# Eight small products of the mLSTM samples: one accumulation in one column tile, against four column tiles at once with the sum on VectorE

## The chip, the cores and the metric

The kernel runs on one core of a Trainium2 chip. The metric is the device time of one execution in microseconds (us), as the median of several timed runs. One execution was also recorded by the hardware profiler; everything said about where the time goes comes from that one trace. The engines carry the names PE (TensorE's matmuls), PEld (TensorE's weight loads), DVE (VectorE), ACT (ScalarE), POOL (GpSimd) and SP (the queue that issues most loads).

## What is computed

The program is one inference step of a two-layer decoder, for a prompt of 512 tokens and for eight separate samples of one token each. Layer 1 has an mLSTM mixer with four heads. For a sample, a head keeps a state C0 of 128 x 256. The part of the reference that the change touches, with t = 1 for the samples and b = 8, is:

```python
def mlstm_chunk(q, k, v, ig, logf, C0, n0, m0):
    ...
    s = jnp.einsum('bhtd,bhsd->bhts', q, k) * w
    num = g[..., None] * jnp.einsum('bhtd,bhde->bhte', q, C0) + jnp.einsum('bhts,bhse->bhte', s, v)
    den = g * jnp.einsum('bhtd,bhd->bht', q, n0) + jnp.sum(s, axis=-1)
    h = num / jnp.maximum(jnp.abs(den), jnp.exp(-m))[..., None]
    ...
    C = g_last[..., None, None] * C0 + jnp.einsum('bhs,bhsd,bhse->bhde', w_last, k, v)
```

Each sample has its own query and its own state, so the product of query and state is eight products of a 1 x 128 row with a 128 x 256 matrix, per head. After the mixer come an output projection, a layer norm, a mixture of 16 experts, a second layer norm and a gate, all on prompt and samples together.

## The kernel before

The mixer of layer 1 is the method `odd`. Its input projection runs as a stream of products `ws_steps`: the weights come in blocks of 128 output columns, ScalarE makes a rounded copy of each block (L137) and VectorE the remainder (L138), and TensorE runs 48 matmuls of 128 x 256 or 128 x 264 on them (L234). Everything else of the mixer is written as Python generators that are advanced once per block (`later`, `advance`), so that their instructions lie between the matmuls of the stream. The tile framework then orders the instructions of each engine by its own plan of when operands come free. Each engine takes its instructions strictly in that order.

`slots` sets which generator is put in when: for each head h it issues the two blocks of v, then `scores(h + 1)` and `sample_head(h, cin)`, and the blocks of o in between. `head(h)` is the prompt's part: for four chunks it computes hs (L1804, L1808, L1809) and updates the prompt's state C (L1811, L1813, and L1815 for the first chunk), and `norm_h` normalizes it (L1837 to L1848; POOL takes a power at L1845). `ocons` applies the gate (L1857, L1858).

`sample_head(h, cin)` is the samples' part, and the place of the change. `cin` holds the eight states of one head, 128 partitions (d) by eight samples by 256. `qm` (L1929) holds for each sample b a 128 x 8 matrix with the query of sample b in column b and zeros elsewhere. Line 1937 multiplies the eight of them with the eight states and lets them accumulate in one PSUM tile of 8 x 256, so that row b of the result is sample b. Lines 1939 and 1941 scale the result, add the term of the new value, and store `num`, a slice of `nums`. Then line 1949 makes the outer products of key and value and line 1950 updates `cin`, in pairs that share a PSUM tile. PSUM tiles named tps come from a pool of four (`tp`); a tile is given out again when its last reader is done.

`sample_out` follows when all four heads are done: `norm_h` on `nums`, eight transposes of it (L266), the gate (L1967). `mix_all` is the output projection, whose first matmuls L142, L143 and L144 need the split result yh and yl of VectorE's and ScalarE's last products, and split weights (L138).

Of the kernel before, what the change touches and what calls it, by code (L numbers as in the profile page):

```python
# [14 lines left out]
OP = mybir.AluOpType  # L15
# [6 lines left out]
NS = 8  # L22
# [98 lines left out]
class K:  # L121
# [1524 lines left out]
    def odd(self):  # L1646
        tc, nc, A, O = self.tc, self.nc, self.A, self.O
        V, S, G, TE = self.V, self.S, self.G, self.T
# [3 lines left out]
        with tc.tile_pool(name="mz", bufs=1) as mz, tc.tile_pool(name="mx", bufs=1) as mx, tc.tile_pool(name="mx2", bufs=2) as mx2:  # L1652
# [6 lines left out]
            ps = self.acc()  # L1659
            for k in range(8):  # L1660
                for z, (a, b) in enumerate(((self.wgh, self.xh), (self.wgh, self.xl), (self.wgl, self.xh))):
                    for q, (t0, t1) in ((ps[:8, 0, 256:512], HALF[0]), (ps[:8, 1, 0:T - 256], HALF[1])):
                        TE.matmul(q, a[:, k, :], b[:, k, t0:t1],
                                  start=(k == 0 and z == 0), stop=(k == 7 and z == 2))
# [4 lines left out]
            ps = self.tp()  # L1669
# [6 lines left out]
            ig, z = ga[:, :, 0:4], ga[:, :, 4:8]  # L1676
# [187 lines left out]
            inter, mm, ws_, gs, ems = (sm[:, z, :] for z in range(1, 6))  # L1864
# [60 lines left out]
            def sample_head(h, cin):  # L1925
                while h not in vdone or len(sdone) < h:
                    yield
                qm = p2.tile([128, 8, 8], F32, name="qm")
                V.tensor_tensor(qm, qT[:, h, None, TP:T].to_broadcast([128, 8, 8]),  # L1929
                                self.c("mask8").rearrange("p (a b) -> p a b", a=8), op=OP.mult)  # L1930

                kk = p2.tile([72, 8, 128], F32R, name="kk", bufs=1)
                V.tensor_tensor(kk, kst[:, None, chunk(h)].to_broadcast([72, 8, 128]).bitcast(F32),
                                self.c("bm")[:72, :, None].to_broadcast([72, 8, 128]), op=OP.mult)
                ps = self.tp()
                for b in range(NS):
                    TE.matmul(ps[:NS, :256], qm[:, b, :], cin[:, b, :], start=(b == 0), stop=(b == 7))
                num = nums[:, h, 0:256]
                V.tensor_scalar(num, ps[:NS, 0:256], gs[:, h:h + 1], None, op0=OP.mult)
                for r in (slice(0, NS), slice(32, 40)):  # L1940
                    V.scalar_tensor_tensor(num, vst[r, h, :].bitcast(F32), sm[:, 6, h:h + 1], num, op0=OP.mult, op1=OP.add)
                for b2 in range(4):
                    if h < 2 or b2 == 0:
                        yield
                    ps = self.tp()
                    for b in range(2):
                        bb = 2 * b2 + b
                        pb = ps[:, b * 256:(b + 1) * 256]
                        TE.matmul(pb, kk[:, bb, :], vst[:, h, :], start=True, stop=True)
                        V.scalar_tensor_tensor(cin[:, bb, :], cin[:, bb, :], gB[:, bb, h:h + 1], pb, op0=OP.mult, op1=OP.add)  # L1950
                G.dma_start(O["C_sample"][0, :, h].rearrange("b p v -> p b v"), cin)
                sdone.add(h)
# [19 lines left out]
            def slots():  # L1972
                self.later(maxima())
                self.later(sample_gates())
                yield from product(4, kcons, 4)
                yield from product(0, qcons, 4)
                self.later(sample_keys())
                self.later(scores(0))
                cins = [sample_load(h) for h in range(2)]
                for n, h in HORD:  # L1980
                    if n == "v":
                        yield from product(8 + 2 * h, vcons)
                        if h < 3:
                            self.later(scores(h + 1))
                        self.later(sample_head(h, cins[h]))
                        if 0 < h < 3:
                            cins.append(sample_load(h + 1))
                    else:
                        yield from product(16 + 2 * h, ocons)
# [57 lines left out]
```

## Time and profile before

| what | value |
|---|---|
| timed runs, median of 3 | 1394.33 us (1392.32 to 1396.9) |
| profiled execution, its own time | 1390.96 us |
| span from first to last instruction in it | 1389.1 us |
| TensorE matmul busy | 1267.9 us (91% of the span) |
| VectorE busy | 858.5 us (62%) |
| ScalarE busy | 627.9 us (45%) |
| GpSimd busy | 254.0 us (18%) |

The profiled execution took 1.9 us more than its span, and 3.4 us less than the median of the timed runs. The busy shares are averages over stages with different limits. The mixer of layer 1 lies between about 740 and 920 us of the span, its output projection begins at 920, and the experts of layer 1 run from about 1005 to 1305.

### The profile page before, as it was taken

How to read it: one execution, taken by the hardware profiler on the slowest of the kernel's cores; microseconds unless marked ns; L12 is line 12 of the kernel's file. 1: busy time of each engine (PE TensorE's matmuls, PEld its weight loads, DVE VectorE, ACT ScalarE, POOL GpSimd, SP SyncE). 2: the span in 40 equal slices, each digit the busy share in tenths (PEclk: the TensorE clock that was granted, in tenths of full speed). 3: DMA queues.
4: the chain of work that ended last, by engine and by line, in shares of the span. 5: the costliest groups of instructions: out<-in, count | busy, mean ns of one | idle time of the engine just before them, and what ended most of it. 6: DMA issues, size and time to landing. Idle time of an engine off the chain costs nothing. (4 is left out here: it accounts for less than half of the span.)

```text
span 1389.1 us, 20899 instructions
## 1 busy us (share of the span) xinstructions
PE 1267.9 (91%) x7884; PEld 967.1 (70%) x7884; DVE 858.5 (62%) x1503; ACT 627.9 (45%) x1053; POOL 254.0 (18%) x242
## 2 busy tenths in 40 slices
PE   8989988995899999888989999999589999999897
PEld 7988876563766655447979988878467565555686
DVE  4699976448976554437554465765788555444572
ACT  3224563224665444337553333233357555444562
POOL 1023312313111211001220000101311112110113
PEclk9999999997999999999999999999889999999999
DMA  8568636864999989997423313483389999999911
GB/s 282 157 221 303 220 137 245 304 240 164 350 359 368 350 301 368 365 363 215 128 86 93 92 46 114 164 324 127 130 304 327 371 361 315 344 371 339 307 56 40
DMA packets 157449, 338.73 MB, mean 244 GB/s; under 512 B 16095, under 2 KB 54459, under 8 KB 153246
## 3 DMA queue, kind: packets, MB, share of 16 engines
q1 hardware_dynamic: 138974, 271.28, 54.9%
q0 software_dynamic: 18224, 65.98, 15.3%
q8 instruction: 64, 1.05, 0.3%
q14 instruction: 43, 0.35, 0.1%
q10 hardware_dynamic: 144, 0.07, 0.0%
HBM read 313.66 MB, written 32.81 MB: 249 GB/s over the span
## 5 line engine op out<-in xcount | busy, mean ns | idle before, releaser
L138 DVE TENSOR_TENSOR w<-w,sh 128x1024 fp32r<-128x1024 f32 x224 | 267.4, 1221 | 123.1 <-ACT sh L137 104.3
L137 ACT CAST sh<-w 128x1024 fp32r<-128x1024 f32 x224 | 227.8, 1048 | 185.1 <-PE acc L234 112.3
L143 PE MATMUL acc<-w,gh 128*128 128x512 f32 x288 | 118.4, 411 | 7.2 <-DVE w L138 6.9
L142 PE MATMUL acc<-sh,gh 128*128 128x512 f32 x288 | 118.1, 410 | 3.4 <-ACT sh L137 3.4
L144 PE MATMUL acc<-sh,gl 128*128 128x512 f32 x288 | 116.6, 405 | 0.0
L1253 PE MATMUL acc<-w,xT 128*64 128x512 f32 x432 | 110.0, 597 | 4.0 <-DMA w<-in_w_exp_up 4.0
L234 PE MATMUL acc<-x2h,w 128*128 128x256 f32 (+1 forms) x384 | 86.9, 288 | 1.6 <-ACT v L1580 0.7
L234 PE MATMUL acc<-xh,sh 128*128 128x256 f32 (+1 forms) x384 | 83.2, 294 | 5.4 <-ACT sh L137 2.2
L234 PE MATMUL acc<-x3h,sh 128*128 128x256 f32 (+1 forms) x384 | 80.9, 290 | 0.0
L234 PE MATMUL acc<-xl,sh 128*128 128x256 f32 (+1 forms) x384 | 79.9, 287 | 0.0
L234 PE MATMUL acc<-xh,w 128*128 128x256 f32 (+1 forms) x384 | 79.2, 287 | 0.7 <-DVE w L138 0.7
L234 PE MATMUL acc<-x3l,sh 128*128 128x256 f32 (+1 forms) x384 | 78.6, 285 | 0.0
L234 PE MATMUL acc<-x3h,w 128*128 128x256 f32 (+1 forms) x384 | 78.1, 283 | 0.0
L1253 PEld LDWEIGHTS acc<-w,xT 128*64 128x64 f32 x432 | 32.5, 136 | 62.4 <-issue 53.0
L143 PEld LDWEIGHTS acc<-w,gh 128*128 128x128 f32 x288 | 55.9, 194 | 24.9 <-DVE w L138 12.4
L1103 POOL DMA_INDIRECT w<-xd,ix x32 | 47.3, 1478 | 140.2 <-DVE gs L1113 80.2
L142 PEld LDWEIGHTS acc<-sh,gh 128*128 128x128 f32 x288 | 55.8, 194 | 18.4 <-ACT sh L137 5.2
L1314 POOL DMA_INDIRECT ya<-y,ix x18 | 29.3, 1626 | 206.9 <-ACT y L1313 206.9
L234 PEld LDWEIGHTS acc<-xh,sh 128*128 128x128 f32 x384 | 61.5, 192 | 7.2 <-ACT raw L391 2.5
L234 PEld LDWEIGHTS acc<-x2h,w 128*128 128x128 f32 x384 | 64.5, 189 | 2.4 <-issue 1.3
L144 PEld LDWEIGHTS acc<-sh,gl 128*128 128x128 f32 x288 | 55.8, 194 | 12.7
L143 PE MATMUL acc<-w,hh 128*128 128x512 f32 x144 | 60.2, 418 | 2.1 <-DVE w L138 2.0
(539 smaller groups left out, 2935.4 us busy)
## 6 DMA issues: line engine op xcount, KB each, us to landing
w<-in_w_exp_gate SPq DMA_DIRECT2D x56, 1024.0 KB
w<-in_w_exp_up SPq DMA_DIRECT2D x50, 1024.0 KB
w<-in_w_exp_down SPq DMA_DIRECT2D x50, 1024.0 KB
wpair<-in_w_exp_up SPq DMA_DIRECT2D x14, 1024.0 KB
w<-in_w_in_even SPq DMA_DIRECT2D x12, 1024.0 KB
w<-in_w_in_odd SPq DMA_DIRECT2D x12, 1024.0 KB
wpair<-in_w_exp_down SPq DMA_DIRECT2D x10, 1024.0 KB
wpair<-in_w_exp_gate SPq DMA_DIRECT2D x8, 1024.0 KB
```

Of the source, the lines that this page charges most:

```text
L137: a = self.S.copy(h, src)
L138: self.sp_last = a, self.V.tensor_sub(l, src, h.bitcast(F32))
L142: self.T.matmul(ps, ah, bh, start=start, stop=False)
L143: self.T.matmul(ps, ah, bl, start=False, stop=False)
L144: self.mm3_last = self.T.matmul(ps, al, bh, start=False, stop=stop)
L234: self.mm_last = self.T.matmul(ps[t], a[:, k, :], b[:, k, t0[t]:t1[t]], start=(k == 0 and i == 0), stop=(k == nk - 1 and i == 2))
L1103: self.gather_last = G.indirect_dma_start(out=xg, out_offset=None, in_=rows2(xd) if small else xd, in_offset=bass.IndirectOffsetOnAxis(ap= ...
L1253: TE.matmul(ps[z * HCAP:(z + 1) * HCAP, :], xT[:, a, hf, :], ws[z][:, a, :], start=(hf == 0 and a == 0), stop=(hf == 1 and a == 3))
L1314: G.indirect_dma_start(out=ya, out_offset=bass.IndirectOffsetOnAxis(ap=ix[:, 0:1], axis=0), in_=y, in_offset=None, bounds_check=T - 1, oob ...
```

## The change

The eight products of a head no longer go to one place. Sample b goes to column tile b mod 4: its 128 x 8 stationary matrix is put into the tile of TensorE's columns that writes PSUM partitions 32(b mod 4) and up. Samples 0 to 3 start the four accumulations, samples 4 to 7 add to them. The PSUM tile then holds four partial results of 8 x 256, at partitions 0, 32, 64 and 96, and their sum is the former result. VectorE scales the first as before, and three new instructions scale and add the others. The number of matmuls stays eight per head.

```diff
                 for b in range(NS):
-                    TE.matmul(ps[:NS, :256], qm[:, b, :], cin[:, b, :], start=(b == 0), stop=(b == 7))
+
+                    z = b % 4 * 32
+                    TE.matmul(ps[z:z + NS, :256], qm[:, b, :], cin[:, b, :], start=(b < 4), stop=(b >= 4))
                 num = nums[:, h, 0:256]
                 V.tensor_scalar(num, ps[:NS, 0:256], gs[:, h:h + 1], None, op0=OP.mult)
+                for z in (32, 64, 96):
+                    V.scalar_tensor_tensor(num, ps[z:z + NS, 0:256], gs[:, h:h + 1], num, op0=OP.mult, op1=OP.add)
```

The lines below move by 2 to 4: L1937, L1939, L1941, L1949 and L1950 are L1939, L1941, L1945, L1953 and L1954 in the changed kernel, and the new sums are L1943. The framework's plan also moves other instructions. Three places follow.

First, VectorE after the sample products of the third head (h = 2). In the kernel before:

```order
L1844 TENSOR_SCALAR hsm<-hsm 128x4
L1846 TENSOR_TENSOR hsm<-hsm 128x4
L1939 TENSOR_SCALAR nums<-tps,ssm 8x256
L1848 TENSOR_SCALAR hs<-hs,hmv,hsm 128x256
L1941 SCALAR_TENSOR_TENSOR nums<-vst,ssm,nums 8x256
L1848 TENSOR_SCALAR hs<-hs,hmv,hsm 128x256
L1941 SCALAR_TENSOR_TENSOR nums<-vst,ssm,nums 8x256
L1792 TENSOR_TENSOR vst<-tps,vst 8x128
L1848 TENSOR_SCALAR hs<-hs,hmv,hsm 128x256 x2
L1837 BN_STATS hst<-nums 8x6
L1838 BN_AGGR hmv<-hst 8x2
L1950 SCALAR_TENSOR_TENSOR w<-w,gB,tps 128x256 x7
```

And in the changed kernel, where the same work begins earlier, between the statistics of the prompt's hs:

```order
L1941 TENSOR_SCALAR nums<-tps,ssm 8x256
L1838 BN_AGGR hmv<-hst 128x2
L1837 BN_STATS hst<-hs 128x6
L1943 SCALAR_TENSOR_TENSOR nums<-tps,ssm,nums 8x256
L1792 TENSOR_TENSOR vst<-tps,vst 8x128
L1943 SCALAR_TENSOR_TENSOR nums<-tps,ssm,nums 8x256
L1838 BN_AGGR hmv<-hst 128x2
L1839 SCALAR_TENSOR_TENSOR hsm<-hs 128x4
L1943 SCALAR_TENSOR_TENSOR nums<-tps,ssm,nums 8x256
L1840 TENSOR_TENSOR hsm<-hsm,em 128x4
L1857 TENSOR_SCALAR sgs<-sg,nw 128x8
L1945 SCALAR_TENSOR_TENSOR nums<-vst,ssm,nums 8x256
```

The scaling and the three sums now stand before the prompt's norm (L1839 to L1848), which before stood ahead of the first scaling but for its last step; the updates of the states (L1954, before L1950), then the copy of C (L1815), still come behind both.

Second, TensorE ahead of the sample products of the fourth head (h = 3). Before:

```order
L1949 MATMUL tps<-vst,kk 128x256
L234 MATMUL acc<-x3l,sh 128x264
L234 MATMUL acc<-x3h,w 128x256
L234 MATMUL acc<-x3h,w 128x264
L234 MATMUL acc<-x3h,sh 128x256
L234 MATMUL acc<-x3h,sh 128x264
L1808 MATMUL tps<-C,qT 128x257
L1811 MATMUL tps<-va,kw 128x257
L1937 MATMUL tps<-w,qm 8x256 x8
```

And in the changed kernel, the last part of it:

```order
L234 MATMUL acc<-x3h,sh 128x264
L234 MATMUL acc<-x3l,sh 128x256
L234 MATMUL acc<-x3l,sh 128x264
L234 MATMUL acc<-x3h,w 128x256
L234 MATMUL acc<-x3h,w 128x264
L1808 MATMUL tps<-C,qT 128x257
L1811 MATMUL tps<-va,kw 128x257
L1939 MATMUL tps<-w,qm 8x256 x8
L234 MATMUL acc<-x3h,sh 128x256
```

Ten matmuls of the stream instead of five stand between the last outer product (L1953, before L1949) and L1808, and counted from the products of the third head it is 16 more; that many fewer stand behind the products of the fourth.

Third, VectorE at the end of the mixer. Before, the samples' norm (L1843 to L1848 on 8 rows) stood far ahead, behind the sums of the fourth head, and this was the end:

```order
L1844 TENSOR_SCALAR hsm<-hsm 128x4
L1857 TENSOR_SCALAR sgs<-sg,nw 128x8
L1846 TENSOR_TENSOR hsm<-hsm 128x4
L1848 TENSOR_SCALAR hs<-hs,hmv,hsm 128x256 x4
L138 TENSOR_TENSOR w<-w,wo_9356 128x1024 x2
L1858 SCALAR_TENSOR_TENSOR yT<-sg,nw,yT 128x512
```

In the changed kernel it reads:

```order
L1844 TENSOR_SCALAR hsm<-hsm 8x4
L1857 TENSOR_SCALAR sgs<-sg,nw 128x8
L1844 TENSOR_SCALAR hsm<-hsm 128x4
L1846 TENSOR_TENSOR hsm<-hsm 128x4
L1846 TENSOR_TENSOR hsm<-hsm 8x4
L1848 TENSOR_SCALAR hs<-hs,hmv,hsm 128x256 x4
L1848 TENSOR_SCALAR nums<-nums,hmv,hsm 8x256 x4
L138 TENSOR_TENSOR w<-w,wo_9368 128x1024 x2
L1858 SCALAR_TENSOR_TENSOR yT<-sg,nw,yT 128x512
```

The samples' norm has moved to the very end, between the prompt's norm and the weight split (L138) that the output projection waits for; its statistics (L1837, L1838 on 8 rows) and one gate (L1858) have moved into the stretch just before, too.

## Rows read from the trace of the kernel before

**Rows 1.** The page: busy time, share of the span and instructions.

```profile
span 1389.1 us, 20899 instructions
PE 1267.9 (91%) x7884; PEld 967.1 (70%) x7884; DVE 858.5 (62%) x1503; ACT 627.9 (45%) x1053; POOL 254.0 (18%) x242
```

**Rows 2.** Busy by stretch: length, engines with instructions, granted clock, DMA share, GB/s.

```profile
880.00:900.00 20.00, 20.00 (x126) 14.42 (x125) 17.07 (x49) 4.09 (x9) 2.54 (x3) 1.00 0.58 185
900.00:920.00 20.00, 19.88 (x156) 18.97 (x155) 13.25 (x41) 6.35 (x12) 3.56 (x4) 1.00 0.79 277
...
1060.00:1100.00 40.00, 38.54 (x205) 25.88 (x205) 29.08 (x32) 25.32 (x29) 6.50 (x5) 1.00 1.02 368
```

**Rows 3.** Waits of PE, 740 to 925 us: total, times, longest.

```profile
PE acc L144 <- DVE yl L138: 2.7, 1, 2.7
```

**Rows 4.** PE timeline (start, us, instructions), first head's products; weight loads of L1937.

```profile
798.66 3.62 PE L1937 MATMUL tps<-w,qm 128*8 128x256 f32 x16
...
802.55 0.41 PE L234 MATMUL acc<-x3l,sh 128*128 128x256 f32 x2
802.80 0.40 PE L234 MATMUL acc<-x3h,w 128*128 128x256 f32 x2
...
L1937 PEld LDWEIGHTS tps<-w,qm x64: 85/90/90, 798.7 to 897.3; 128*8 128x8 f32 x64
L1937 PE MATMUL tps<-w,qm x64: 379/379/384, 798.7 to 897.5; 128*8 128x256 f32 x64
```

**Rows 5.** Layer 0's attention of the samples (L669, L677), timeline.

```profile
220.66 0.16 PEld L669 LDWEIGHTS tps<-w,a 128*32 128x32 f32 x8 [0.44 <-ACT a L639]
220.66 1.92 PE L669 MATMUL tps<-w,a 128*32 128x512 f32 x16 [0.34 <-ACT a L639]
221.12 0.13 PEld L669 LDWEIGHTS tps<-w,a 128*32 128x32 f32 x4 [0.30 <-issue]
...
225.14 1.02 PE L677 MATMUL tps<-mk,eb 128*8 128x512 f32 x2
```

**Rows 6.** DVE timeline behind the products of the first head.

```profile
802.85 0.97 DVE L1941 SCALAR_TENSOR_TENSOR nums<-vst,ssm,nums 8x256 f32<-8x256 f32 x2
```

**Rows 7.** Third head: timeline of PE and DVE, and busy time of one stretch.

```profile
884.97 0.16 DVE L1846 TENSOR_TENSOR hsm<-hsm 128x4 f32<-128x4 f32 x1 [1.22 <-POOL hsm L1845]
...
889.29 2.71 DVE L1950 SCALAR_TENSOR_TENSOR w<-w,gB,tps 128x256 f32<-128x256 f32 x6 [0.61 <-PE tps L1949]
...
892.65 0.42 DVE L1815 COPY C<-tps 128x257 f32<-128x257 f32 x1
...
893.28 0.60 PE L1808 MATMUL tps<-C,qT 128*128 128x257 f32 x2
...
880.87:892.65 11.78, 11.78 (x79) 9.27 (x78) 9.37 (x32) 3.72 (x8) 1.60 (x2) 1.00 0.54 179
```

**Rows 8.** End of the mixer: timeline of DVE, POOL and PE.

```profile
899.43 0.42 DVE L1837 BATCH_NORM_STATS2 hst<-nums 8x6 f32<-8x256 f32 x1
901.75 1.37 DVE L1848 TENSOR_SCALAR nums<-nums,hmv,hsm 8x256 f32<-8x256 f32 x4
912.79 1.03 POOL L1845 TENSOR_TENSOR hsm<-hsm,cst 128x4 f32<-128x4 f32 x1 [0.37 <-DVE hsm L1844]
918.61 1.04 PE L266 MATMUL tps<-cst,hs 128*128 128x128 f32 x8
918.81 2.36 DVE L138 TENSOR_TENSOR w<-w,wo 128x1024 fp32r<-128x1024 f32 x2 [3.35 <-PE acc L234]
921.09 0.75 DVE L1858 SCALAR_TENSOR_TENSOR yT<-sg,nw,yT 128x512 f32<-128x512 f32 x1
```

**Rows 9.** Busy by stretch at the start of the output projection.

```profile
922.00:924.00 2.00, 0.00 (x0) 0.00 (x0) 2.00 (x5) 2.00 (x4) 0.08 (x1) 0.86 0.99 347
...
928.00:930.00 2.00, 2.00 (x6) 1.52 (x6) 1.97 (x3) 0.00 (x0) 0.00 (x0) 0.50 1.04 391
...
932.00:934.00 2.00, 2.00 (x11) 1.61 (x10) 0.69 (x1) 0.49 (x1) 0.00 (x0) 1.00 1.05 387
```

## The prediction, made before the changed kernel was run

> **What bounds the kernel now.** I read the page first: TensorE is busy 1267.9 of 1389.1 us [rows 1]. That is only an average, so I then asked for stretches. In the mixer of layer 1, where the change lies, TensorE is busy 20.00 and 19.88 of 20 us at the full clock, and VectorE 17.07 and 13.25 [rows 2]. The list of waits says the same in another way: between 740 and 925 us, TensorE's matmuls show one wait, 2.7 us for VectorE's yl at the start of the output projection [rows 3]. So TensorE's own work sets the pace, with VectorE close behind it from 880 us on. What is saved there is passed on if nothing later has a fixed start. The experts keep the DMA queues full (share 1.02 at 1060 to 1100 us) with TensorE busy 38.54 of 40 us [rows 2]; but their loads wait for buffers that TensorE frees, so that stage slides as a whole, and I count no loss there.
>
> **What the products cost now.** The reader is to see in [rows 4] that eight matmuls are 16 instructions (each float32 product is two passes), that one instruction lasts 379 ns, and that the 16 take 3.62 us. From start to start that is (3.62 - 0.38)/15 = 0.216 us: they run one after the other. There are four such bursts (64 instructions).
>
> **What four tiles cost.** The kernel has a row for it: the samples' attention of layer 0 (L669) sends its float32 products to four column tiles in the same pattern, 32 columns each and 512 wide. There, 16 instructions take 1.92 us. The two instructions of L677, also 512 wide and in one tile, take 1.02 us with 594 ns each, so one costs 0.43 us; 16 in a row would take 15 x 0.43 + 0.59 = 7.0 us, and four rounds of four take 3 x 0.43 + 0.59 = 1.88 us, which is what stands there [rows 5]. The change's products differ in two ways: 8 columns instead of 32, which can only shorten the load, and 256 elements instead of 512, which shortens a round to 0.216 us. A load of eight columns takes 85 to 90 ns [rows 4], less than a round, so I expect it to stay hidden, and a burst of 3 x 0.216 + 0.38 = 1.03 us, with some 0.02 for the offsets between tiles: 1.05. **Saved: 3.62 - 1.05 = 2.57 us per head, 10.3 us in all.** Bounds: nothing, if the tiles do not overlap at this size; 10.3 if all of it reaches the end.
>
> The Trainium skill speaks against this: "TensorE: Matmul & The Clock Gate", Part 3, says that a weight load overlaps running matmuls only where its row group differs, and all four tiles here use all rows. This trace disagrees: behind L669's first eight loads, four more stand at 221.12, inside the burst that runs from 220.66 to 222.58 [rows 5]. By the rule the burst would be longer; that is a rival below.
>
> **What VectorE pays.** Twelve new sums, 8 x 256, with one input in PSUM. The nearest rows are L1941 (two dependent ones in 0.97 us, so 0.50 from one to the next) and L1950, which reads PSUM (six in 2.71 us, 0.45 from one to the next) [rows 6, 7]. I take 0.45, since the order puts other instructions between most of them: 1.35 us per head, 5.4 in all (6.0 by the other row). For the first two heads the order gives TensorE 48 and 44 stream matmuls (0.12 us each by the pairs of [rows 4], so more than 5 us) before it needs another PSUM tile or the new num, so the sums are hidden. If that cover were gone they would cost 1.35 each.
>
> The **third head** has no such cover. From 880.87 to 892.65 us VectorE is busy 9.37 of 11.78 us; at the end it copies C (L1815), and L1808 of TensorE cannot start before that (893.28) [rows 7]. With 1.35 added it needs 10.7, and it still waits for POOL's power in the middle (1.22 now), so C comes after about 11.8 us again: TensorE's 2.57 us of this head are not collected at L1808. Behind the waiting L1808 stand the fourth head's products. But the new order has put 16 stream matmuls in front of it, 16 x 0.12 = 1.93 us of work that is done during the wait. Lost here: 2.57 - 1.93 = **0.64 us** (bounds 0 and 2.57).
>
> The **end of the mixer**. Before, VectorE had 3.35 us to spare ahead of the split at 918.81, which starts 0.2 us after TensorE has finished the stream (918.61) [rows 8]. The new order fills that hole: the samples' statistics (0.42), six small steps (0.16 each, as L1846 in [rows 7]), a second power on POOL (1.03, in series with the first), the scaling of nums (1.37) and one gate (0.75). That is 0.42 + 0.96 + 1.03 + 1.37 + 0.75 = 4.5 us; some of the small ones lie in the shadow of POOL, so I take 4.2. 4.2 - 3.35 = **0.85 us** late, and what is late next is the chain of split, gate and yl on which L144 waits: its wait grows from 2.7 to about 3.5 us. Bounds: 0 and 4.2.
>
> **The clock.** In that wait the granted clock falls: 0.86 at 922 to 924, where PE runs nothing, then 0.50 (1.2 of 2.4 GHz), six matmuls in 2 us instead of eleven at 932 to 934 [rows 9]. So each us at the low clock loses 5/11, or 0.45; from the end of the wait, after 924, to about 930 I take 5.5 us of it, which cost 2.5. The wait stays and grows a little, so I leave the cost as it is; it could vanish (2.5 us won) or double.
>
> **The sum.** 10.3 - 0.64 - 0.85 = 8.8 us. On the profiled execution (1389.1 span, 1390.96 in all) that gives 1382.2. The median of the timed runs lies 3.4 above the profiled one, so for timed runs I say 1394.3 - 8.8 = **1385.5 us**, 0.63% less. A measurement of this kernel tells about 0.3%, or 4.2 us, from no change.
>
> **Rivals.**
> VectorE takes over (0.17): heads three and four yield nothing, because VectorE, at 17.07 of 20 us plus two heads' sums (2.7), is full while TensorE needs 5.1 us less [rows 2]; only 5.1 us of the first two heads remain, less 0.85: 4.3 us, 1390.0. Against it: the stream matmuls moved forward, and VectorE's 13.25 of 20 us after 900. The Trainium skill, "TensorEngine Tiling (Array Packing)", PSUM Bottleneck, states this danger as a rule: tiling speeds up TensorE but not the emptying of PSUM, which may then bound. No row of before can settle it.
>
> Loads stand in the open (0.06): each round of four waits for its four loads one after the other, 4 x 0.09 + 0.216 = 0.58 us, a burst of 2.5 us, 1.1 saved per head; 4.4 less 1.5 for VectorE's delays: 1391.4. That is what the page's row-group rule would do. Against it: [rows 5].
>
> The change doesn't do what it says (0.03): tiles of 8 columns run one after the other, TensorE gains nothing and VectorE's delays stay: about 1395.
>
> Slower (0.04): the moved samples' norm at the end lengthens the wait before L144 so far that the low clock lasts through the output projection. With 0.45 lost of each us it decides from 8.8/0.45 = 20 us of further low clock, and with 35 us, half of the projection, the time would be 1394.3 - 8.8 + 16 = 1401. For it: the clock does fall in just this wait. Against it: it recovered within 6 us.
>
> The rest (0.70) is the forecast, whose own range is 1382 to 1389: from 8.8 by the clock's 2.5 and the full 10.3 on one side, by the larger losses on VectorE on the other.
>
> **Chances and range.** Faster by over 0.3%: the forecast and half of the first rival, 0.78. Within 0.3%: the other half and the two cases without much gain, 0.17. Slower: 0.05. The range 1380 to 1391 reaches from the full saving on the lowest of the timed runs (1392.3 - 10.3 - 2.5, rounded up) to the first rival with a microsecond more; about 0.2 is left out.
>
> **What would show it.** L1939 must be 16 instructions in about 1.05 us, in four rounds 0.216 us apart; a burst of 2.5 or 3.6 us makes the prediction wrong at its first step. L1943 should stand at 0.45 to 0.50 from one to the next. In the third head, L1815 should end about 5 us earlier than before, not 7.7. The split of wo should start about 9 us earlier, with hardly any wait for TensorE in front of it, and L144's wait should be near 3.5 us with the clock at 0.50 behind it. If the end of the mixer comes 9 us earlier and the end of the span does not, a later stage had a fixed start, which I excluded.

## The result, and the profile after

The changed kernel takes **1383.81 us** (median of 7 runs, 1378.11 to 1389.26), against 1394.33 before (7 runs, 1392.32 to 1397.70). The medians are 10.5 us apart, or 0.75%; the forecast was 1385.5 us, 8.8 us or 0.63% less. The ratio on record, which is not the quotient of these two medians, is 0.9936 with a 95% interval of 0.9915 to 0.9957, that is 0.64% less. The profiled execution took 1380.0 us.

The page after, answering to [rows 1]; TensorE's matmuls are as many as before, VectorE has 12 instructions more:

```profile
span 1378.2 us, 20912 instructions
PE 1263.3 (92%) x7884; PEld 967.4 (70%) x7884; DVE 863.5 (63%) x1515; ACT 628.7 (46%) x1053; POOL 254.0 (18%) x242
```

To see where the span's 10.9 us come from, I divide it at four points that both traces have: the first sample product (798.66 before, 797.58 after), the transposes of the last head's hs behind the stream (L266, 918.61 and 908.82), the first L144 (924.55 and 914.84), and the end. I call the stretch between the first two **M**. Only M holds edited work.

| stretch | before | after | difference |
|---|---|---|---|
| start to the first sample product | 798.66 | 797.58 | -1.08 |
| M: to the transposes behind the stream | 119.95 | 111.24 | -8.71 |
| to the first L144 | 5.94 | 6.02 | +0.08 |
| to the end | 464.5 | 463.3 | -1.2 |

The first line is spread: in the 14 profiles of this study the first product stands anywhere from 796.1 to 806.2 us, though TensorE runs the same 4699 instructions up to there in all of them, in the same order but for two that are exchanged in four kernels. M hardly varies with the execution: two kernels that differ only behind M both have 111.24. So M is the measure for the experiments, and the timed ratios stand beside it. What the forecast of 8.8 us speaks of is M and the stretch behind it, together 8.63 us; the other 2.3 of the 10.9 are the spread and a shorter low clock (below).

**The burst.** The timeline of the first head after the change (start, duration, engine, instruction; in brackets the idle time before it and what ended it):

```profile
797.58 1.05 PE L1939 MATMUL tps<-w,qm 128*8 128x256 f32 x16
...
799.11 0.47 DVE L1941 TENSOR_SCALAR nums<-tps,ssm 8x256 f32<-8x256 f32 x1
...
799.75 1.51 DVE L1943 SCALAR_TENSOR_TENSOR nums<-tps,ssm,nums 8x256 f32<-8x256 f32 x3
801.29 0.98 DVE L1945 SCALAR_TENSOR_TENSOR nums<-vst,ssm,nums 8x256 f32<-8x256 f32 x2
```

The sixteen instructions take 1.05 us instead of 3.62 [rows 4], and so do the other three bursts. Inside one, the starts come in four groups, 0.22 us apart, and 7 ns apart within a group. The three sums take 1.51 us, 0.51 from one to the next; the forecast took 0.45.

**The third head.** The timelines of VectorE and TensorE, to be read against [rows 7]:

```profile
881.16 0.48 DVE L1954 SCALAR_TENSOR_TENSOR w<-w,gB,tps 128x256 f32<-128x256 f32 x1
881.56 0.16 DVE L1844 TENSOR_SCALAR hsm<-hsm 128x4 f32<-128x4 f32 x1
881.63 0.47 DVE L1954 SCALAR_TENSOR_TENSOR w<-w,gB,tps 128x256 f32<-128x256 f32 x1
881.69 0.38 PE L1953 MATMUL tps<-vst,kk 72*128 72x256 f32 x1 [0.21 <-DVE w L1954]
...
882.94 0.16 DVE L1846 TENSOR_TENSOR hsm<-hsm 128x4 f32<-128x4 f32 x1 [0.84 <-POOL hsm L1845]
883.02 0.47 DVE L1954 SCALAR_TENSOR_TENSOR w<-w,gB,tps 128x256 f32<-128x256 f32 x1
883.41 1.38 DVE L1848 TENSOR_SCALAR hs<-hs,hmv,hsm 128x256 f32<-128x256 f32 x4
883.64 0.67 PE L1804 MATMUL tps<-va,w 128*128 128x257 f32 x2 [0.71 <-DVE w L1954]
...
887.30 0.42 DVE L1815 COPY C<-tps 128x257 f32<-128x257 f32 x1
```

The reader is to see a queue. The third update (L1954) is behind L1846, which waits 0.84 us for GpSimd's power. Until that update has read its PSUM tile, TensorE has no tile for L1804 and waits 0.71 us. These two waits of TensorE, 0.21 and 0.71, are the only ones in M longer than 60 ns; before, there was one of 0.12. The section on the change puts all updates behind the prompt's norm. In the trace two of them stand ahead of its wait (881.16 and 881.63), one between L1846 and L1848, and five behind L1848.

**The end of the mixer.** VectorE and TensorE, against [rows 8] and [rows 3]:

```profile
906.45 0.15 DVE L1846 TENSOR_TENSOR hsm<-hsm 8x4 f32<-8x4 f32 x1 [0.83 <-POOL hsm L1845]
906.53 1.37 DVE L1848 TENSOR_SCALAR hs<-hs,hmv,hsm 128x256 f32<-128x256 f32 x4
907.83 1.37 DVE L1848 TENSOR_SCALAR nums<-nums,hmv,hsm 8x256 f32<-8x256 f32 x4
909.12 2.34 DVE L138 TENSOR_TENSOR w<-w,wo 128x1024 fp32r<-128x1024 f32 x2
...
914.84 0.73 PE L144 MATMUL acc<-wo,yl 128*128 128x512 f32 x2 [2.75 <-DVE yl L138]
```

The split of wo follows the samples' norm without a pause and begins 0.30 us after TensorE's transposes (908.82), against 0.20 before. TensorE's wait for yl is 2.75 us, against 2.67.

**The clock behind that wait.** Busy time by stretch: length, then PE, PEld, DVE, ACT and POOL, granted clock, DMA share, GB/s; against [rows 9]:

```profile
912.00:914.00 2.00, 0.10 (x1) 0.00 (x0) 2.00 (x5) 2.00 (x3) 0.29 (x1) 1.00 1.04 396
...
916.00:918.00 2.00, 2.00 (x7) 1.51 (x6) 2.00 (x3) 0.00 (x0) 0.00 (x0) 0.50 1.04 377
918.00:920.00 2.00, 2.00 (x8) 1.57 (x6) 1.97 (x3) 0.00 (x0) 0.00 (x0) 0.65 1.04 396
920.00:922.00 2.00, 2.00 (x10) 1.63 (x9) 1.41 (x3) 0.62 (x1) 0.00 (x0) 1.00 1.04 390
```

TensorE idles as long as before, and the clock falls as before, but the low stretch is shorter. From the first L144 to the tenth after it 8.19 us pass, against 9.20. That is 1.0 of the 1.2 us that the table shows behind the first L144.

### The profile page after: what moved, and what is told of

The parts are those of the page before. It is cut to its first block, busy times and chain, and to the rows that moved or that the text cites. A ratio compares the mean times of both kernels' runs of the same rounds, so it can differ in the third digit from the quotient of the medians.

```text
span 1378.2 us, 20912 instructions
## 1 busy us (share of the span) xinstructions
PE 1263.3 (92%) x7884; PEld 967.4 (70%) x7884; DVE 863.5 (63%) x1515; ACT 628.7 (46%) x1053; POOL 254.0 (18%) x242
## 3 DMA queue, kind: packets, MB, share of 16 engines
q8 instruction: 64, 1.05, 0.3%
## 5 line engine op out<-in xcount | busy, mean ns | idle before, releaser
L138 DVE TENSOR_TENSOR w<-w,sh 128x1024 fp32r<-128x1024 f32 x224 | 267.3, 1221 | 117.5 <-ACT sh L137 98.8
L144 PE MATMUL acc<-sh,gl 128*128 128x512 f32 x288 | 117.1, 407 | 0.0
L144 PEld LDWEIGHTS acc<-sh,gl 128*128 128x128 f32 x288 | 56.4, 196 | 13.0
L234 PEld LDWEIGHTS acc<-xh,w 128*128 128x128 f32 x384 | 61.7, 194 | 1.4 <-DVE w L138 1.3
```

The costliest lines, as they stand in the source:

```text
L138: self.sp_last = a, self.V.tensor_sub(l, src, h.bitcast(F32))
L144: self.mm3_last = self.T.matmul(ps, al, bh, start=False, stop=stop)
L234: self.mm_last = self.T.matmul(ps[t], a[:, k, :], b[:, k, t0[t]:t1[t]], start=(k == 0 and i == 0), stop=(k == nk - 1 and i == 2))
```

## The experiments

Four tiles save 4 x 2.57 = 10.28 us of TensorE, so with nothing lost M would be 119.95 - 10.28 = 109.67. It is 111.24: **1.57 us are missing.** The theory was that VectorE's sums cost them, in the third head; the first rivals were that each head loses a little, and that the sums have no part in it. TensorE runs the same 850 instructions in M in all 14 kernels, in different orders. The waits longer than 60 ns make 0.92 of the 1.57 us; the rest shows in no wait of the list. In the table, "missing" is M less what the bursts alone would leave (109.67 with four tiles, 114.81 with four tiles in two heads, 113.07 with two tiles, where the bursts were measured to save 6.88).

| kernel | first product, transposes | M | missing | time ratio to before (95%) |
|---|---|---|---|---|
| before | 798.66, 918.61 | 119.95 | 0 | 1 |
| changed | 797.58, 908.82 | 111.24 | 1.57 | 0.9936 (0.9915 to 0.9957) |
| e1_no_sums | 804.97, 917.16 | 112.19 | 2.52 | 0.9947 (0.9921 to 0.9972) |
| e2_sums_only | 797.51, 918.60 | 121.09 | 1.14 | 1.0013 (0.9992 to 1.0033) |
| e4_heads01 | 800.25, 915.58 | 115.33 | 0.52 | 0.9952 (0.9924 to 0.9981) |
| e5_heads23 | 799.92, 916.41 | 116.49 | 1.68 | 0.9985 (0.9963 to 1.0007) |
| e3_two_tiles | 798.25, 914.58 | 116.33 | 3.26 | 0.9974 (0.9951 to 0.9998) |
| e6_scale_act | 796.14, 906.56 | 110.42 | 0.75 | 0.9929 (0.9908 to 0.9951) |
| e7_fill_wait | 796.49, 907.73 | 111.24 | 1.57 | 0.9916 (0.9884 to 0.9948) |
| g0_before_first | 799.73, 921.24 | 121.51 | 1.56 | 0.9989 (0.9959 to 1.0019) |
| g1_after_first | 799.10, 911.35 | 112.25 | 2.58 | 0.9928 (0.9901 to 0.9954) |
| g2_two_first | 806.21, 922.06 | 115.85 | 2.78 | 0.9966 (0.9940 to 0.9991) |
| g3_nosums_first | 805.66, 919.36 | 113.70 | 4.03 | 0.9944 (0.9920 to 0.9967) |
| b1_act_fill | 797.26, 907.70 | 110.44 | 0.77 | 0.9901 (0.9872 to 0.9930) |

**Sums left out (e1_no_sums).** The four tiles stay, the three sums go:

```diff
-                for z in (32, 64, 96):
-                    V.scalar_tensor_tensor(num, ps[z:z + NS, 0:256], gs[:, h:h + 1], num, op0=OP.mult, op1=OP.add)
```

> The changed kernel without its three sums per head, so the query-state products of samples 1 to 3 and 5 to 7 are left out of the output; the four tiles stay. Measured in the trace: the stretch M from the first sample product of head 0 to the first transpose of the last head's hs behind the stream (119.95 us before, 111.22 after). Theory (TensorE bounds, and the 1.55 us that are missing from the full 10.28 are VectorE's 12 sums in the third head): M = 109.7 to 110.0, no wait over 0.2 us of TensorE for L1954's successor, and some 1.3 us less than the changed kernel in time, about 1382.5. Rival (the third head's wait comes from the power on GpSimd and the number of PSUM tiles whatever the sums do): M stays at 110.9 to 111.3.

Both missed. With less work on VectorE, M became longer. The timeline of its third head (L1951 is L1953 of the changed kernel, L1952 is L1954):

```profile
888.09 0.17 DVE L1844 TENSOR_SCALAR hsm<-hsm 128x4 f32<-128x4 f32 x1
...
888.58 0.64 PE L1951 MATMUL tps<-vst,kk 72*128 72x256 f32 x4
889.48 0.16 DVE L1846 TENSOR_TENSOR hsm<-hsm 128x4 f32<-128x4 f32 x1 [1.22 <-POOL hsm L1845]
...
889.68 1.38 DVE L1848 TENSOR_SCALAR hs<-hs,hmv,hsm 128x256 f32<-128x256 f32 x4
890.98 2.22 DVE L1952 SCALAR_TENSOR_TENSOR w<-w,gB,tps 128x256 f32<-128x256 f32 x5
891.50 0.39 PE L1951 MATMUL tps<-vst,kk 72*128 72x256 f32 x1 [1.32 <-DVE w L1952]
```

Without the sums the framework plans another order: the whole norm, with its wait for GpSimd, now stands ahead of all updates, and TensorE waits 1.32 us for the first of them (0.82 more in the second head, where the changed kernel has two updates ahead of the norm's wait). The work on VectorE in the last two heads, from the products of the third to the split of wo, in the changed kernel:

```profile
874.56:909.12 34.56, 33.64 (x266) 30.15 (x266) 29.74 (x92) 9.26 (x19) 6.04 (x7) 1.00 0.69 251
```

and without the sums:

```profile
882.78:917.36 34.58, 33.14 (x265) 30.18 (x265) 27.69 (x87) 9.25 (x19) 6.64 (x7) 1.00 0.70 250
```

VectorE is busy 2.05 us less, and the stretch is as long. So it is not the amount of work on VectorE that sets its length, in these two orders.

**Sums alone (e2_sums_only).** The kernel before, with three sums per head that read the one tile again:

```diff
                 V.tensor_scalar(num, ps[:NS, 0:256], gs[:, h:h + 1], None, op0=OP.mult)
+                for z in (0, 0, 0):
+                    V.scalar_tensor_tensor(num, ps[z:z + NS, 0:256], gs[:, h:h + 1], num, op0=OP.mult, op1=OP.add)
```

> The kernel before (one column tile), with three more sums per head that read the same eight PSUM rows again, so the query-state product is counted four times in the output. Theory: with the slow products TensorE paces all heads, VectorE's 1.4 us per head are hidden but in the third head: M between 119.95 and 120.6, time within 1 us of before. Rival (VectorE is already close to the bound from 880 us on): M grows by 1.4 us or more, to 121.4 to 122.8, the time to about 1396.

M grew by 1.14 us, between the two, and the time by 0.13%; the interval of this ratio holds 1. TensorE waits 0.42 us for an update (third head) and 0.82 for C (L1808 behind L1813, fourth head). The sums are not free, even under slow products.

**Half of the heads (e4_heads01, e5_heads23).** `nt` is 4 for the heads named and 1 for the others:

```diff
-                    z = b % 4 * 32
-                    TE.matmul(ps[z:z + NS, :256], qm[:, b, :], cin[:, b, :], start=(b < 4), stop=(b >= 4))
+                    nt = 4 if h < 2 else 1
+                    z = b % nt * 32
+                    TE.matmul(ps[z:z + NS, :256], qm[:, b, :], cin[:, b, :], start=(b < nt), stop=(b >= NS - nt))
...
-                for z in (32, 64, 96):
+                for z in (32, 64, 96)[:nt - 1]:
```

> Four tiles and three sums for heads 0 and 1 only; heads 2 and 3 as before. Theory (all of the loss lies in the third head): M = 119.95 - 5.14 = 114.8 (up to 115.1), time about 1389.2. Rival (each head loses a little): M about 115.6, time 1390.

> Four tiles and three sums for heads 2 and 3 only; heads 0 and 1 as before. Theory: 5.14 saved less the 1.55 of the third head: M = 116.2 to 116.5, a wait of TensorE of 0.7 to 1.0 us in the third head, time about 1390.7. Rival (each head loses a little): M about 115.6. Rival (VectorE is the bound in both last heads): M 118 or more.

Heads 2 and 3 alone lack 1.68 us, with waits of 0.21 and 0.71 in the third head, as in the changed kernel, and with the same 14.35 us from the third head's products to the fourth's: the theory's place holds. Heads 0 and 1 alone still lack 0.52, between the theory and the rival; the third head's order is as before there, and the waits of 0.12 and 0.33 are in the fourth, behind the prompt's C and hs.

**Two tiles (e3_two_tiles).** `z = b % 2 * 32`, `start=(b < 2)`, `stop=(b >= 6)`, and one sum.

> Two column tiles instead of four, one sum per head. Theory (a round of tiles takes as long as one product, 0.216 us from start to start): a burst of eight rounds, 7 x 0.216 + 0.38 = 1.89 us, 1.73 saved per head, 6.9 in all, and with one sum hardly any loss in the third head: M = 113.0 to 113.6, time about 1387.6. Rival (the loss in the third head is the same with one sum as with three): M about 114.4.

The bursts are as long as was expected:

```profile
798.25 1.90 PE L1939 MATMUL tps<-w,qm 128*8 128x256 f32 x16
```

They save 6.88 us in all. Only 3.62 of it arrive, and M missed both figures. The list of waits of TensorE from 790 to 930 us (total, times, longest):

```profile
PE acc L144 <- DVE yl L138: 2.7, 1, 2.7
PE tps L1953 <- DVE w L1954: 2.5, 2, 1.3
PE tps L1808 <- DVE C L1813: 0.7, 1, 0.7
```

Two of the waits are again the updates' tiles, in the second head as well as in the third. One sum gives a longer wait than three. As in e1_no_sums, the whole norm stands ahead of all updates in the third head, its wait for GpSimd included (L1846 at 885.31, the updates from 886.80).

**The first scaling on ScalarE (e6_scale_act).**

```diff
-                V.tensor_scalar(num, ps[:NS, 0:256], gs[:, h:h + 1], None, op0=OP.mult)
+                S.activation(num, ps[:NS, 0:256], AF.Copy, scale=gs[:, h:h + 1])
```

> The changed kernel with the first scaling of each head (L1941) on ScalarE instead of VectorE. Theory (VectorE's own time in the third head is what TensorE waits for): 0.47 us less on VectorE there, so M = 110.6 to 110.9. Rival (VectorE waits in that head for GpSimd's power anyway): M = 111.1 to 111.3. Rival (ScalarE is busy with a cast when the products are done, and the sums start later): M 111.5 or more.

M fell to 110.42, a little further than the theory said; 0.75 us are missing. TensorE's waits in the third head are 0.17 and 0.51. With this edit VectorE has less to do and the updates start nearer to the outer products, and this run alone does not tell the one from the other.

**The idle time filled (e7_fill_wait).** Twelve matmuls whose result nobody reads, in the wait for yl (`i` is the layer, `hf` the half of the columns):

```diff
+                if i and m == k == 0 and hf:
+                    junk = self.tp()
+                    for _ in range(12):
+                        TE.matmul(junk, yh[:, 0, :], h, start=True, stop=True)
                 self.mm3(acc[hf][:, 0, :], yh[:, k % 4, :], yl[:, k % 4, :], h, l, k == 0, k == 7)
```

> The changed kernel with twelve more matmuls of 128 x 512 into an unused PSUM tile, in the stretch in which TensorE waits for yl at the start of the output projection; their result is not read, the output is unchanged. Theory (the idle time is what lowers the granted clock behind it): the clock stays at 1.00 from 912 to 920 us, L144 starts as late as before after the split (5.7 us), and the time from L144's start to the end falls by 2 us, from 463.4 to 461.4; time about 1381.8. Rival (the clock falls for another reason, as the loads that begin there): 0.50 and 0.65 stay at 916 to 920 us, and the time stays. Rival (the extra matmuls slow VectorE or push L144 back): L144 starts later and the time grows.

Its timeline of TensorE:

```profile
909.96 2.90 PE L930 MATMUL tps<-wo,yh 128*128 128x512 f32 x12
...
913.76 0.73 PE L144 MATMUL acc<-wo,yl 128*128 128x512 f32 x2 [0.44 <-DVE yl L138]
```

and its stretches behind it:

```profile
914.00:916.00 2.00, 2.00 (x10) 1.60 (x10) 2.00 (x3) 0.00 (x0) 0.00 (x0) 1.00 1.04 391
916.00:918.00 2.00, 2.00 (x10) 1.64 (x9) 1.97 (x3) 0.00 (x0) 0.00 (x0) 1.00 1.02 379
```

The clock stays at full, with the same loads running, and the split ends as late as before (6.03 us from the transposes to L144). From the first L144 to the tenth after it 6.60 us pass, against 8.19 in the changed kernel and 9.20 before: the low clock behind the idle time costs 1.6 and 2.6 us. Of the 2 us that were expected from the first L144 to the end, 0.4 show (462.9 us against 463.3), because the rest behind the tenth took 456.3 us against 455.1; over all kernels here this rest lies between 453.4 and 456.3. The timed ratio is 0.9916; its interval holds the changed kernel's 0.9936.

**Updates first (g1, g2, g3, g0).** After e1_no_sums the theory had fallen, and I formed another: what is missing is the planned order, updates queued behind the norm's wait for GpSimd. One edit in four kernels puts the outer products and updates early in the plan:

```diff
-                        TE.matmul(pb, kk[:, bb, :], vst[:, h, :], start=True, stop=True)
-                        V.scalar_tensor_tensor(cin[:, bb, :], cin[:, bb, :], gB[:, bb, h:h + 1], pb, op0=OP.mult, op1=OP.add)
+                        with self.tc.high_priority():
+                            TE.matmul(pb, kk[:, bb, :], vst[:, h, :], start=True, stop=True)
+                            V.scalar_tensor_tensor(cin[:, bb, :], cin[:, bb, :], gB[:, bb, h:h + 1], pb, op0=OP.mult, op1=OP.add)
```

> The changed kernel; the outer products and state updates (L1953, L1954) get a high priority in the framework's plan, so that in the third head they stand on VectorE ahead of the norm's step that waits for GpSimd's power. All sums stay. M is the stretch from the first sample product to the transposes behind the stream. New theory (what is missing from the full 10.28 us is the plan: updates queued behind that wait keep PSUM tiles from TensorE): M falls from 111.24 to 109.8 to 110.5, and the waits of 0.2 and 0.7 us in the third head go. Rival (the amount of work on VectorE): M stays at 111.0 to 111.4. Rival (the wait only moves, to the step that now stands behind the updates): M 111 or more with a new wait of 0.5 us or more elsewhere.

> Two column tiles and one sum per head, with the same high priority for outer products and updates. New theory: the waits of 1.18, 1.34 and 0.70 us behind L1954 and C go, M falls from 116.33 to 113.1 to 113.8, about what four tiles would give less 3.4 us. Rival (two tiles save less than their burst shows): M stays above 115.5.

> Four tiles without the three sums (the products of samples 1 to 3 and 5 to 7 are left out of the output), with the same high priority. New theory: the waits of 0.82 and 1.32 us go, M falls from 112.18 to 109.7 to 110.3, so that the sums themselves cost 0 to 0.5 us against the changed kernel with the same priority. Rival (the amount of work on VectorE): 1.2 us or more below that kernel. Rival (the plan is not it): M stays near 112.

> The kernel before with the same high priority, a control. It has only one wait of 0.12 us in the stretch, so the new theory gives M = 119.7 to 120.1 and the time of before. Rival (the priority makes any kernel faster): M below 119.

In g1, g2 and g3 the waits for the updates' tiles are gone, as the new theory said. M did not follow. In g1 it rose to 112.25, in g3 to 113.70; g2 gained 0.5. In g1 the wait moved, as the second of its rivals said. The list of waits of g1, 790 to 930 us:

```profile
PE acc L144 <- DVE yl L138: 2.7, 1, 2.7
PE tps L1808 <- DVE C L1813: 1.1, 1, 1.1
PE tps L1808 <- DVE C L1815: 0.4, 1, 0.4
```

and the timeline of g3 in the fourth head, where the longest of them stands:

```profile
901.13 0.15 DVE L1846 TENSOR_TENSOR hsm<-hsm 8x4 f32<-8x4 f32 x1 [1.12 <-POOL hsm L1845]
...
901.31 1.37 DVE L1848 TENSOR_SCALAR nums<-nums,hmv,hsm 8x256 f32<-8x256 f32 x4
...
902.74 1.40 DVE L1858 SCALAR_TENSOR_TENSOR yT<-sg,nw,yT 128x512 f32<-128x512 f32 x2
...
904.07 0.47 DVE L1809 SCALAR_TENSOR_TENSOR hs<-tps,gg,hs 128x257 f32<-128x257 f32 x1
904.46 0.46 DVE L1813 SCALAR_TENSOR_TENSOR C<-C,gL,tps 128x257 f32<-128x257 f32 x1
905.07 0.67 PE L1808 MATMUL tps<-C,qT 128*128 128x257 f32 x2 [1.89 <-DVE C L1813]
```

Here it is the samples' norm, again with a wait for GpSimd, that stands ahead of the prompt's C. And behind this wait of 1.89 us the granted clock falls inside M, as in no other kernel here (stretches of g3, columns as above):

```profile
906.00:908.00 2.00, 2.00 (x10) 1.80 (x9) 2.00 (x6) 1.87 (x3) 0.61 (x1) 0.56 0.44 162
908.00:910.00 2.00, 2.00 (x13) 2.00 (x12) 1.24 (x3) 0.00 (x0) 0.00 (x0) 0.59 0.16 66
910.00:912.00 2.00, 2.00 (x19) 2.00 (x18) 1.93 (x9) 0.00 (x0) 0.68 (x1) 1.00 0.00 0
```

TensorE has 10 and 13 instructions in 2 us where it has 19 at the full clock. By these rows that is about 1.6 us, an estimate; with the wait it makes 3.5 of the 4.03 us missing. So g3's long M is no sign that leaving out the sums makes M longer.

The control g0 missed both of its figures and lost 1.56 us of its own. In all four an outer product also stands in the middle of the second head's burst, in g0 and g2 two of them. In g1 this burst takes 1.89 us instead of 1.05, and 0.61 of the 1.01 us by which its M exceeds the changed kernel's lie ahead of the third head's products, where it has no wait longer than 60 ns. So the priority is no cure, and "updates first" is not the whole of the cause.

**Both edits that helped (b1_act_fill).** The diffs of e6_scale_act and e7_fill_wait together.

> The changed kernel with both edits that helped: the first scaling of each head on ScalarE, and twelve unread matmuls in TensorE's wait for yl. Theory (the two add, since they lie in different stretches): M = 110.43 as with the scaling alone, a gap of about 0.35 us before L144, the clock at 1.00 behind it and the tenth L144 after the first 6.6 us later (8.2 to 9.2 without the fill); 0.990 of the time before, about 1380. Rival (they cancel, because the shorter mixer leaves the loads of wo or of the experts later than TensorE): M or the time to L144 grows, and the ratio stays at 0.992 to 0.993.

In the trace they add: M is 110.44, the wait for yl 0.33 us, the tenth L144 after the first 6.61 us later, the ratio 0.9901 (0.9872 to 0.9930), 1376.41 us against 1390.0 for the kernel before on the same chip. It has the lowest ratio of all that ran, though its interval overlaps the changed kernel's.

## Why the prediction was right, step by step

- **The burst: right.** 1.05 us expected and measured, in four rounds; 2.57 us per head saved on TensorE. The rival of loads in the open (2.5 us a burst) is out. The Trainium skill's row-group rule ("TensorE: Matmul & The Clock Gate", Part 3) would have given that longer burst; at 8 columns and 256 elements the trace disagrees with it, as [rows 5] did at 32 and 512.
- **First two heads hidden: right here.** From the first products to the second 40.84 us pass, 2.47 less than before, and to the third 36.14, 2.49 less: 0.17 of 5.14 lost. e3_two_tiles shows that the cover is no property of the edit, since its second head waits 1.18 us.
- **Third head: right place, too small, and by another wait.** I expected 0.64 us lost, because C would come as long after the products as before, with L1808 waiting for it. C came 12.74 us after them (874.56 to 887.30), against 12.05 before (880.60 to 892.65 [rows 7]), 0.69 later. Together with the 0.64 that makes 1.33, and 1.34 is what the stretch from the third products to the fourth shows: 14.35 us against 13.64 - 2.57 + 1.94 = 13.01 (1.94 for the 16 stream matmuls moved into it). The wait stands at L1953 and L1804, for PSUM tiles that the updates hold, and not at L1808. But L1808 starts only 0.17 us after the copy of C ends (0.21 before), so that without these waits C might have held it: which of the two sets the stretch, this trace does not tell. The order showed most of the updates behind the norm's wait; I followed C alone, and not the four tiles.
- **End of the mixer: VectorE's time met by luck, the lateness too large.** 0.85 us late was expected, 0.10 measured (0.30 after the transposes against 0.20), and the wait for yl is 2.75 us and not 3.5. VectorE reached the split 111.54 us after the first product; the sum gave 120.15 - 8.8 = 111.35. Two errors cancel in that. The third head lost 0.70 us more than the sum had; and from the fourth head's products on VectorE took 20.22 us to the split, 0.68 less than the 20.90 of the sum (24.36 to the transposes before, less 2.57 and the 1.94 moved away, plus 0.20 and 0.85). TensorE came to the transposes 0.93 us later than the sum had it (111.24 against 119.95 - 10.28 + 0.64 = 110.31), so that little of VectorE's delay was left to see. In all, 1.49 us of losses stood in the sum, 0.64 of them in M; measured are 1.65, 1.57 of them in M. The total fits, its parts do not.
- **The clock: the size left alone was wrong by 1 us.** I kept its cost at 2.5. It was 2.6 before and 1.6 after, by e7_fill_wait's 6.60 us at the full clock. That is inside the stated bounds, it rests on one execution of each kernel, and it is a part of the result that the edit did not aim at.
- **Nothing later had a fixed start: right.** Behind the first L144 the program took no longer than before.
- **VectorE takes over: not so.** The stretch of the last two heads is as long with 27.69 us of VectorE's work as with 29.74. The rule of the Trainium skill on this danger ("TensorEngine Tiling (Array Packing)", PSUM Bottleneck) gave that rival; in the traces here the waits follow VectorE's queue order. That its load has no part is not shown: e6_scale_act, with one step less per head on VectorE, has an M that is 0.82 us shorter.

What stays open is whether the sums alone cost anything in the changed kernel. Every edit made the framework plan anew, and M moved by up to 2.5 us with the plan (1.57 us missing in the changed kernel, 4.03 in g3, about 1.6 of them by the clock). A kernel with the changed kernel's order and without its sums was not made, and no order was found in which all of 10.28 us arrives. An untested rival is the number of PSUM tiles: a fifth one in the pool, which would let TensorE go on while an update stands in VectorE's queue, was not tried.

## What to carry to other kernels

Small products that each fill a few columns can share TensorE's columns, and a burst of them then costs its rounds (here 3.62, 1.90 and 1.05 us for sixteen, eight and four): look in the trace for the same pattern elsewhere in the kernel and scale it by rounds. Before counting the saving as time, follow each queue behind the edited step, above all the PSUM tiles that a queued reader holds while it stands behind a wait for a third engine. Where a scheduler orders the instructions, an experiment that removes work also changes the order, so compare the waits and the granted clock of each variant before calling the difference the price of the work. A wait of TensorE can cost more than its length, as the one of 1.89 us in g3 did.

## What the runs showed of the hardware that was not expected

After an idle time of TensorE of the same length (2.66 to 2.76 us), the stretch at a granted clock of 0.50 (1.2 of 2.4 GHz) that follows is not equally long. From the first L144 to the tenth after it the kernels took 9.20 us (before), 9.25 (e3_two_tiles) and 9.36 (e5_heads23), or 7.95 to 8.19 in the other nine without the fill, and 6.60 and 6.61 with it. In g3 the clock also fell behind a wait of 1.89 us, to 0.56 and 0.59 in the next two stretches of 2 us; behind the waits of 1.32 us in e1_no_sums and 1.34 in e3_two_tiles it stayed at 1.00. What decides between the two lengths was not found; about 1 us of any comparison of single executions hangs on it here.
